# Row fetches of the mixer stage queued behind the vector instruction before them and spaced by 7.5 instead of 11; two kinds of matrix products pinned to their place

## The chip, the cores and the metric

One core of a Trainium2 chip runs the whole program. The metric is the device time of one execution in microseconds (us). The kernel before takes 3400.1 us, the median of 3 runs (3396.47 to 3403.27).

The core has a matrix engine (TensorE, PE in the profile; its weight loads are PEld), a vector engine (VectorE, DVE), an activation engine (ScalarE, ACT), a general engine (GpSimd, POOL) and SyncE (SP), which here issues most DMAs. Each engine works through its own queue in order. What one engine needs of another it waits for by a semaphore. GpSimd issues the indirect DMAs of this kernel, which fetch table rows by an index.

## The reference

One layer on 1024 tokens of width 1024: a mixer (a gated recurrence and a short convolution, merged by gates), and then PEER, a retrieval of single-neuron experts. Cut to what matters here:

```python
x = x + merged @ w_out[l]                       # the mixer's end
h = rmsnorm(x, norm_ffn_g[l])
q = (h @ w_query).reshape(t, 8, 2, 128)
v1, i1 = lax.top_k(q[:, :, 0] . keys1, 16)      # per head, two halves
v2, i2 = lax.top_k(q[:, :, 1] . keys2, 16)
cand_s = v1[..., :, None] + v2[..., None, :]
top_s, top_pos = lax.top_k(cand_s, 16)          # 16 experts a head, 128 a token
idx = take_along_axis(cand_i, top_pos)          # of 16384 experts
gate = softmax(top_s)
act = gelu(einsum('thkd,td->thk', expert_u[idx], h))
out = einsum('thk,thkd->td', gate * act, expert_v[idx])
x = x + out
return rmsnorm(x, norm_final_g)
```

So each token needs 128 rows of `peer_u`, each multiplied with its activation vector and summed, and 128 rows of `peer_v`, each scaled and added up.

## The kernel before

The 1024 tokens are 8 tiles of 128, or 4 groups G0 to G3 of 256. The program has two stages and an end.

The mixer stage. For each group there are generators: `front` (norm, transposes, convolution), `recurrence` (4 head pairs, each with one cumulative scan on VectorE, L574, and the decays on GpSimd, L705 to L709), `gates_a`, `gates_b`, `post` (merge, output projection with its residual add L639, second norm, query projection, the scores and the first top-16) and `picks_of` (the second top-16, the softmax and the expert numbers of a tile). With G2 begins `all_gates`: for the four tiles 2 to 5 it spreads the picked gates over all 16384 experts by one-hot products, eight tokens at a time: four or five wide VectorE instructions (L1000 to L1003) make the operands, and `spread` multiplies them (L976, L977).

The dense stage. Tiles 2 to 5 go through all experts with dense products: `first` (products with the `peer_u` blocks, L296 and L299, gelu, times the gates, L1032), and `second` with the `peer_v` blocks (products L287 to L289 and L1057, sums L1068). The picks of G3 run beside its beginning.

The rows. Tiles 0, 1, 6 and 7 are done by row instead (`gather`): GpSimd issues one indirect DMA (L902) for expert k of 128 tokens at once, 128 rows of 4 KB. For a `u` row block VectorE multiplies it with the activations and sums (L932, with an accumulator read behind it); for a `v` row block it scales and adds (L938). Below, one such fetch with its one VectorE instruction is called a row fetch, and there are 4 x 128 x 2 = 1024 of them. They are put into blocks of 32 experts, the `v` of a block beside the `u` of the next. `gather` yields after every second expert, so a step of it is mostly four row fetches, u, v, u, v. In the mixer stage four buffers (`mem_g`) take the rows, and from the dense stage on there are eight (`mem_e` too). A fetch waits for its buffer, that is for the VectorE instruction that read it four (eight) fetches ago.

What sets the order. `together` runs the generators of the mixer against a clock of its own, which counts the columns of the products traced so far; a generator that yields a number sleeps for so long on that clock. `paced` (L378) steps the rows: one step, then a sleep of `ROW_STEP`, 11.0 of those clock units. `interleave` (L430) deals out the steps that are left over the dense stage, in proportion to the products traced, out of `ROW_STEPS` = 290; it does so within `issue_after(mine[-1])`, which queues the VectorE instructions of the step behind the last VectorE instruction of the dense work. What is still left comes behind the dense stage. A list scheduler then reorders the instructions of each engine by its own idea of when operands are ready; an edge made by `issue_after` or `keep_in_program_order` is an order that it must keep, and no wait on the chip. `issue_after` binds only instructions on the engine of the one that it is given, so the fetches on GpSimd are not bound by it.

Of the kernel before, what the change touches and what calls it, by code (L numbers as in the profile page):

```python
# [22 lines left out]
P = 128  # L23
# [35 lines left out]
W_SHARE = 0.5  # L59
ROWS_AT_ONCE = 4  # L60
T_REC, T_GATES, T_W, T_POST, T_FRONT, T_PICK = 92.0, 6.4, 55.0, 92.0, 170.0, 10.89
T_SOON, T_ROWS, ROW_STEP = 300.0, 1e4, 11.0
FROM = 2
T_GB, T_FIRST = 27, 40.0
ROW_STEPS, T_DENSE = 290, 1330.0
# [60 lines left out]
class Layer:  # L126
# [251 lines left out]
    def paced(self, rows):  # L378

        while 0 not in self.idx:  # L380
            yield 1
        while not self.stop:
            next(rows)
            self.row_steps += 1
            yield ROW_STEP

# [434 lines left out]
    def pick(self, tile_no, top, topi, mem):  # L821

        nc = self.nc
# [55 lines left out]
        yield PICK  # L879
        ps = self.ps()  # L880
        for i, src in enumerate((i12[:, 0], i12[:, 1], gate)):
            nc.tensor.transpose(ps[:, i * P:(i + 1) * P], src, self.ident)

        pt = self.view(self.M.pt_kb + 2 * DENSE.index(tile_no), [4, P, 2], F16)
        pairs = ps[:, :3 * P].unsqueeze(2).broadcast_to([P, 3 * P, 2])
# [71 lines left out]
    def all_gates(self, tiles, last):  # L957

        nc, M = self.nc, self.M
        T = 8  # L960
        while not last.conv:
            yield 1
        ix = self.view(M.ix_kb, [NKEYS], F16)
        nc.vector.tensor_copy(ix, self.iota)
        ix = ix.rearrange("p (k d) -> p k d", d=2).unsqueeze(1).broadcast_to([P, T, NKEYS // 2, 2])
        todo = []

        def spread():

            o2, q0, q1, dst, out = todo.pop(0)  # L970
            for h in range(2):
                ps = self.ps()
                for j in range(4):
                    tk = 4 * h + j
                    o = ps[:, j * P:(j + 1) * P]
                    nc.tensor.matmul(o, o2[:, tk, :], q0[:, tk, :], start=True, stop=False)  # L976
                    nc.tensor.matmul(o, o2[:, tk, :], q1[:, tk, :], start=False, stop=True)  # L977
                nc.scalar.copy(dst[:, :, 4 * h:4 * h + 4].rearrange("p a t -> p t a"),
                               ps.rearrange("p (t a) -> p t a", t=4))
            if out:  # L980
                nc.sync.dma_start(*out)
                yield OUT

        for i_, t in enumerate(tiles):
            while t not in self.pt:
                yield 1
            pt = self.pt[t]
            for tb in range(P // TB):
                stage = M.stage.take([NKEYS, TB])
                for u in range(0, TB, T):  # L990
                    def along(i):
                        t_ = tb * TB + u
                        return pt[:, i, t_:t_ + T, :].unsqueeze(2).broadcast_to([P, T, NKEYS // 2, 2])

                    def twos(x):
                        return x.rearrange("p t (k d) -> p t k d", d=2)

                    o2, o1 = M.o2.take([T, NKEYS], F16), M.o1.take([T, NKEYS], F16)
                    q0, q1 = M.q0.take([T, NKEYS], F16), M.q1.take([T, NKEYS], F16)
                    nc.vector.tensor_tensor(twos(o2), ix, along(1), op=ALU.is_equal)  # L1000
                    nc.vector.tensor_tensor(twos(o1), ix, along(0), op=ALU.is_equal)
                    nc.vector.tensor_tensor(twos(q0), twos(o1), along(2), op=ALU.mult)
                    self.either(Q_SHARE).tensor_tensor(twos(q1), twos(o1), along(3), op=ALU.mult)  # L1003
                    yield SPREAD if todo else 0
                    if todo:
                        yield from spread()
                    todo.append((o2, q0, q1, stage[:, :, u:u + T],
                                 (self.wd[i_ * (P // TB) + tb], stage) if u + T == TB else None))
        yield SPREAD
        yield from spread()  # L1010

    def dense(self, M, n0, n):
# [170 lines left out]
```

## Time and profile before

| | us |
|---|---|
| median of 3 runs | 3400.1 |
| the profiled execution | 3427.02 |
| its span, first to last instruction | 3425.3 |
| PE busy | 2839.6 |
| DVE busy | 2769.9 |
| POOL busy | 1750.8 |
| ACT busy | 999.3 |

The span has three parts, by what the engines do: the mixer stage to about 1686 us, where the first gates of the dense stage are multiplied; the dense stage to 3102 us, where TensorE ends; and the end to 3425 us, in which VectorE still works through row fetches. In a table of stretches the number in brackets behind an engine's busy time is its count of instructions; PEclk is the granted share of TensorE's full clock; then come the mean busy share of the 16 DMA engines and what they moved.

### The profile page before, as it was taken

The page shows a single profiled execution, that of the slowest core. Times are in us where ns is not written, and L with a number is a line of the kernel's source. Part 1 is how long each engine was busy: PE and PEld are TensorE (multiplying, and loading weights), DVE is VectorE, ACT ScalarE, POOL GpSimd, SP SyncE. Part 2 cuts the span into 40 slices and gives each one's busy share as a digit, 9 for nine tenths or more (in the row PEclk, how much of TensorE's full clock was granted, in tenths as well). Part 3 has the DMA queues.
Part 4 walks back from the last instruction along what each step waited for, and adds up shares of the span by engine and source line. Part 5 has one row for each costly group of instructions (what it writes and reads, how often), then busy time and mean ns, then how long its engine had stood idle before and what let it go on. Part 6 is the DMA issues. An engine that isn't in the chain of part 4 may idle for free.

```text
span 3425.3 us, 42902 instructions
## 1 busy us (share of the span) xinstructions
PE 2839.6 (83%) x14956; PEld 2389.3 (70%) x14956; DVE 2769.9 (81%) x5515; ACT 999.3 (29%) x1528; POOL 1750.8 (51%) x1460
## 2 busy tenths in 40 slices
PE   8999998598975799978689999999999999992000
PEld 7887887487864688867578888888888888881000
DVE  2232489868899865789999999999899999989787
ACT  3232232323312354234323333333333333330000
POOL 0001036665546401220467677676677776657875
PEclk9998999798997899988799999999999999996555
DMA  6434558898886754454689999999899999989998
GB/s 199 139 108 122 162 182 294 274 337 310 299 302 211 279 193 145 149 202 157 223 273 354 356 337 344 333 343 336 317 357 337 336 343 341 341 313 335 321 354 297
DMA packets 321721, 938.01 MB, mean 274 GB/s; under 512 B 29280, under 2 KB 103520, under 8 KB 319456
## 3 DMA queue, kind: packets, MB, share of 16 engines
q0 software_dynamic: 147456, 536.94, 43.5%
q1 hardware_dynamic: 174048, 398.32, 34.0%
q8 instruction: 118, 1.93, 0.2%
q14 instruction: 99, 0.81, 0.1%
HBM read 889.01 MB, written 46.14 MB: 273 GB/s over the span
## 4 chain that ended last, share of the span: by engine, by line
PE 61%; DVE 18%; issue 7%; DMA 7%; POOL 5%; ACT 1%; SPq 0%; POOLq 0%; DVEq 0%; ACTq 0%
PE ps L260 16%; PE ps L1057 15%; PE ps L296 13%; PE ps L299 6%; DMA mem_g<-in_peer_v,idx 4%; DVE mem_g L938 3%; DVE mem_g L932 2%; DVE mem_z L864 2%; POOL mem_g L902 2%; DMA mem_g<-in_peer_u,idx 2%; PE ps L740 2%; PE ps L288 2%; PE ps L287 2%; PE ps L289 2%; PE ps L633 1%
## 5 line engine op out<-in xcount | busy, mean ns | idle before, releaser
L260 PE MATMUL ps<-mem_h,mem_w 128*128 128x256 f32 x3584 | 840.7, 392 | 2.1 <-DVE mem_a L516 1.0
L260 PEld LDWEIGHTS ps<-mem_h,mem_w 128*128 128x128 f32 x3584 | 696.4, 197 | 103.9 <-DVE mem_a L516 1.3
L1057 PE MATMUL ps<-mem_v,mem_ph 128*128 128x512 f32 x2304 | 571.8, 398 | 22.4 <-ACT mem_ph L247 13.1
L902 POOL DMA_INDIRECT mem_g<-in_peer_u,idx x324 | 397.0, 1225 | 261.9 <-DVE mem_g L932 120.9
L902 POOL DMA_INDIRECT mem_g<-in_peer_v,idx x308 | 394.1, 1280 | 262.5 <-DVE mem_g L938 163.7
L1057 PEld LDWEIGHTS ps<-mem_v,mem_ph 128*128 128x128 f32 x2304 | 436.3, 190 | 128.2 <-ACT mem_ph L247 14.0
L296 PE MATMUL ps<-mem_ht,mem_s 128*128 128x512 f32 x2048 | 508.1, 390 | 0.2 <-ACT mem_ht L247 0.2
L932 DVE SCALAR_TENSOR_TENSOR mem_g<-mem_g 128x1024 f32<-128x1024 f32 x324 | 429.0, 1327 | 37.0 <-DMA mem_g<-in_peer_u,idx 33.3
L938 DVE SCALAR_TENSOR_TENSOR mem_g<-mem_g 128x1024 f32<-128x1024 f32 x308 | 411.6, 1336 | 51.1 <-DMA mem_g<-in_peer_v,idx 47.5
L296 PEld LDWEIGHTS ps<-mem_ht,mem_s 128*128 128x128 f32 x2048 | 384.2, 188 | 83.6 <-DVE mem_z L1068 0.5
L705 POOL TENSOR_TENSOR mem_y<-mem_y 128x128 f32<-128x128 f32 x96 | 48.3, 504 | 552.7 <-DVE mem_y L574 552.6
L902 POOL DMA_INDIRECT mem_e<-in_peer_v,idx x204 | 267.5, 1311 | 115.8 <-DVE mem_g L938 69.1
L247 ACT ACTIVATE mem_s<-mem_raw 128x512 fp32r<-128x512 f32 x256 | 160.9, 630 | 509.1 <-PE ps L296 489.8
L902 POOL DMA_INDIRECT mem_e<-in_peer_u,idx x188 | 240.1, 1277 | 112.5 <-DVE mem_e L932 61.9
L938 DVE SCALAR_TENSOR_TENSOR mem_g<-mem_e,mem_g 128x1024 f32<-128x1024 f32 x204 | 269.1, 1319 | 17.9 <-DMA mem_e<-in_peer_v,idx 16.1
L299 PE MATMUL ps<-mem_ht,mem_s 128*128 128x512 f32 x1024 | 273.6, 389 | 0.0
L248 POOL TENSOR_TENSOR mem_s<-mem_raw,mem_s 128x512 fp32r<-128x512 f32 x128 | 189.7, 1483 | 140.6 <-ACT mem_s L247 137.2
L932 DVE SCALAR_TENSOR_TENSOR mem_e<-mem_e,mem_g 128x1024 f32<-128x1024 f32 x188 | 242.9, 1297 | 18.0 <-DMA mem_e<-in_peer_u,idx 17.9
L863 POOL TENSOR_TENSOR mem_z<-mem_z 128x800 f32<-128x800 f16 x64 | 124.8, 1950 | 186.9 <-DVE mem_z L861 176.7
L299 PEld LDWEIGHTS ps<-mem_ht,mem_s 128*128 128x128 f32 x1024 | 192.2, 188 | 39.9
L1032 DVE TENSOR_TENSOR mem_z<-mem_z 128x512 f32<-128x512 f32 x128 | 171.7, 1342 | 33.4 <-ACT mem_z L1030 32.8
L247 ACT ACTIVATE mem_ph<-mem_z 128x512 fp32r<-128x512 f32 x128 | 80.9, 632 | 310.6 <-DVE mem_z L1032 303.7
(194 smaller groups left out, 4216.3 us busy)
## 6 DMA issues: line engine op xcount, KB each, us to landing
mem_w<-in_w_in SPq DMA_DIRECT2D x160, 512.0 KB
mem_raw<-in_peer_ut SPq DMA_DIRECT2D x128, 512.0 KB
mem_z<-in_peer_v SPq DMA_DIRECT2D x128, 512.0 KB
mem_w<-in_w_query SPq DMA_DIRECT2D x64, 512.0 KB
wd<-mem_a SPq DMA_DIRECT2D x16, 2048.0 KB
mem_z<-wd SPq DMA_DIRECT2D x32, 1024.0 KB
mem_w<-in_w_out SPq DMA_DIRECT2D x32, 512.0 KB
mem_w<-in_w_conv SPq DMA_DIRECT2D x32, 256.0 KB
```

Source lines behind the costliest of these rows:

```text
L247: self.nc.scalar.activation(hi, src, AF.Copy)
L248: self.either(pool_share).tensor_tensor(lo, src, hi.bitcast(F32), op=ALU.subtract)
L260: self.nc.tensor.matmul(ps, w[:, kk, :], act[:, kk, :], start=kk == 0, stop=kk == k - 1)
L287: mm(ps, lh, rh, start=first, stop=False, **kw)
L296: mm(ps, w[kk][0], act[part][:, kk, :], start=kk == part == 0, stop=False)
L299: mm(ps, w[j][1], act[0][:, j, :], start=False, stop=j == k - 1)
L863: nc.gpsimd.tensor_tensor(pr, eq, ci[:, hd, :].unsqueeze(2).broadcast_to([P, NCAND, TOPK]), op=ALU.mult)
L902: nc.gpsimd.indirect_dma_start(out=r, out_offset=None, in_=a[table], in_offset=bass.IndirectOffsetOnAxis(ap=self.idx[t][:, k:k + 1], axis=0))
L932: nc.vector.scalar_tensor_tensor(u, u, 1.0, h2, op0=ALU.mult, op1=ALU.mult, accum_out=wt[:, k:k + 1])
L938: nc.vector.scalar_tensor_tensor(acc, v, wt[:, k:k + 1], acc, op0=ALU.mult, op1=ALU.add)
L1032: nc.vector.tensor_tensor(gv, gv, w4[c // 4][:, :, c % 4, :], op=ALU.mult)
L1057: nc.tensor.matmul(acc[t][hf], pp[c][i][:, tk], vp[c][:, k, 512 * hf:512 * hf + 512], start=c == 0 and i == 0 and k == 0, stop=c == NKEYS ...
```

## The change

`ROW_STEP` falls from 11.0 to 7.5. Each step of the rows in `paced` now runs within `issue_after(last)`, with `last` the VectorE instruction traced just before. The three transposes of a dense tile's picks (L882 before, L884 after) and the first product of each half of `spread` (L976 before, L978 after) are pinned by `keep_in_program_order` behind the TensorE instruction traced before them.

```diff
-T_SOON, T_ROWS, ROW_STEP = 300.0, 1e4, 11.0
+T_SOON, T_ROWS, ROW_STEP = 300.0, 1e4, 7.5
...
         while not self.stop:
-            next(rows)
+            last = next(i for i in reversed(self.traced()) if i.engine == mybir.EngineType.DVE)
+            with self.tc.issue_after(last):
+                next(rows)
             self.row_steps += 1
             yield ROW_STEP
...
-            nc.tensor.transpose(ps[:, i * P:(i + 1) * P], src, self.ident)
+            self.tc.keep_in_program_order(nc.tensor.transpose(ps[:, i * P:(i + 1) * P], src, self.ident))
...
-                    nc.tensor.matmul(o, o2[:, tk, :], q0[:, tk, :], start=True, stop=False)
+                    mm = nc.tensor.matmul(o, o2[:, tk, :], q0[:, tk, :], start=True, stop=False)
+                    if j == 0:
+                        self.tc.keep_in_program_order(mm)
                     nc.tensor.matmul(o, o2[:, tk, :], q1[:, tk, :], start=False, stop=True)
```

The lines behind L382 move by two, those behind L975 by four (L932 is L934, L938 is L940, L1032 is L1036, L1068 is L1072).

Counted over the whole order of VectorE's queue, row fetches stand as follows (the scans L574 mark the head pairs, four a group):

| row fetches on VectorE | before | after |
|---|---|---|
| ahead of the 7th scan | 7 | 4 |
| 7th to 13th scan | 219 | 148 |
| 13th scan to the first gate product of the dense stage (L1032) | 20 | 200 |
| from there to the last sum of the dense stage (L1068) | 578 | 587 |
| behind it | 200 | 85 |

VectorE's queue behind the 8th scan, in the recurrence of G1. First before, from the end of the decays (L721) on; L750 to L758 are the scores of a head pair, L776 its state:

```order
L721 TENSOR_TENSOR mem_y<-mem_y 128x256
L932 SCALAR_TENSOR_TENSOR mem_g<-mem_g 128x1024
L938 SCALAR_TENSOR_TENSOR mem_g<-mem_g 128x1024
L750 TENSOR_TENSOR mem_y<-ps,c_masks 128x256
L932 SCALAR_TENSOR_TENSOR mem_g<-mem_g 128x1024
L750 TENSOR_TENSOR mem_y<-ps,c_masks 128x256
L938 SCALAR_TENSOR_TENSOR mem_g<-mem_g 128x1024
L776 SCALAR_TENSOR_TENSOR st_126<-st_125,el,ps 64x64 x2
L758 TENSOR_TENSOR mem_y<-mem_y 128x2x32
L932 SCALAR_TENSOR_TENSOR mem_g<-mem_g 128x1024
L758 TENSOR_TENSOR mem_y<-mem_y 128x4x16
L938 SCALAR_TENSOR_TENSOR mem_g<-mem_g 128x1024
```

And the same place now:

```order
L723 TENSOR_TENSOR mem_y<-mem_y 128x256
L752 TENSOR_TENSOR mem_y<-ps,c_masks 128x256 x2
L760 TENSOR_TENSOR mem_y<-mem_y 128x2x32
L760 TENSOR_TENSOR mem_y<-mem_y 128x4x16
L760 TENSOR_TENSOR mem_y<-mem_y 128x8x8
L778 SCALAR_TENSOR_TENSOR st_126<-st_125,el,ps 64x64 x2
L760 TENSOR_TENSOR mem_y<-mem_y 128x16x4
L760 TENSOR_TENSOR mem_y<-mem_y 128x32x2
L760 TENSOR_TENSOR mem_y<-mem_y 128x64
L934 SCALAR_TENSOR_TENSOR mem_g<-mem_g 128x1024 x2
L778 SCALAR_TENSOR_TENSOR st_125<-st_126,el,ps 64x64 x2
```

Six row fetches stood between the pieces of one chain, and now two stand behind them.

VectorE's queue at the first residual adds of G3's `post` (L639, now L641), where the spread of the last dense tiles runs beside it. Before:

```order
L639 TENSOR_TENSOR mem_z<-ps,mem_z 128x512
L864 TENSOR_REDUCE mem_z<-mem_z 128x16
L861 TENSOR_TENSOR mem_z<-iota_x,mem_z 128x800
L1001 TENSOR_TENSOR mem_a<-mem_z 128x1024
L639 TENSOR_TENSOR mem_z<-ps,mem_z 128x512
L1000 TENSOR_TENSOR mem_a<-mem_z 128x1024
L1002 TENSOR_TENSOR mem_o<-mem_a,mem_z 128x1024
L1003 TENSOR_TENSOR mem_o<-mem_a,mem_z 128x1024
```

And now:

```order
L641 TENSOR_TENSOR mem_z<-ps,mem_z 128x512
L1005 TENSOR_TENSOR mem_a<-mem_z 128x1024
L940 SCALAR_TENSOR_TENSOR mem_g<-mem_g 128x1024
L866 TENSOR_REDUCE mem_z<-mem_z 128x16
L863 TENSOR_TENSOR mem_z<-iota_x,mem_z 128x800
L1004 TENSOR_TENSOR mem_a<-mem_z 128x1024
L1006 TENSOR_TENSOR mem_o<-mem_a,mem_z 128x1024
L1007 TENSOR_TENSOR mem_o<-mem_a,mem_z 128x1024
L1004 TENSOR_TENSOR mem_o<-mem_z 128x1024
L934 SCALAR_TENSOR_TENSOR mem_g<-mem_g 128x1024
L641 TENSOR_TENSOR mem_z<-ps,mem_z 128x512
L940 SCALAR_TENSOR_TENSOR mem_g<-mem_g 128x1024
```

Where no row fetch stood, three now stand within these twelve instructions.

TensorE's queue at the transposes of the first dense tile's picks. Before:

```order
L769 MATMUL ps<-mem_y 64x64
L771 MATMUL ps<-mem_y 64x64
L882 MATMUL ps<-c_ident,mem_z 128x128 x3
L260 MATMUL ps<-mem_h_153,mem_w 128x256 x8
L976 LDWEIGHTS mem_a
L976 MATMUL ps<-mem_o,mem_a 128x128
L976 LDWEIGHTS mem_a
L976 MATMUL ps<-mem_o,mem_a 128x128
```

And now:

```order
L771 MATMUL ps<-mem_y 64x64
L773 MATMUL ps<-mem_y 64x64
L884 MATMUL ps<-c_ident,mem_z 128x128 x3
L260 MATMUL ps<-mem_h_153,mem_w 128x256 x8
L978 LDWEIGHTS mem_a
L978 MATMUL ps<-mem_o,mem_a 128x128
L981 LDWEIGHTS mem_a
L981 MATMUL ps<-mem_o,mem_a 128x128
```

The transposes stand at the same place in TensorE's queue (three of the four tiles' have the same number of instructions ahead of them in both kernels, and the second tile's have 28 more). Of the spread's products the two of one token now follow each other, where the first products of several tokens stood together.

## Rows read from the trace of the kernel before

**Rows 1.** The page: busy time of each engine, the span in 40 slices for DVE and the DMA engines, and the chain that ended last by engine.

```profile
PE 2839.6 (83%) x14956; PEld 2389.3 (70%) x14956; DVE 2769.9 (81%) x5515; ACT 999.3 (29%) x1528; POOL 1750.8 (51%) x1460
...
DVE  2232489868899865789999999999899999989787
...
DMA  6434558898886754454689999999899999989998
...
PE 61%; DVE 18%; issue 7%; DMA 7%; POOL 5%; ACT 1%; SPq 0%; POOLq 0%; DVEq 0%; ACTq 0%
```

**Rows 2.** Busy time of the engines by stretch: window, its length, then PE, PEld, DVE, ACT and POOL busy with their counts, PEclk, DMA share, GB/s.

```profile
525.50:1120.00 594.50, 462.96 (x2710) 397.18 (x2709) 520.37 (x1232) 158.92 (x258) 353.27 (x329) 0.87 0.83 291
1120.00:1690.00 570.00, 476.97 (x3236) 415.46 (x3235) 440.65 (x1453) 235.10 (x342) 122.55 (x118) 0.89 0.54 188
1690.00:1800.00 110.00, 99.33 (x414) 79.56 (x412) 109.97 (x124) 33.10 (x48) 75.88 (x52) 0.95 0.80 267
1800.00:3102.00 1302.00, 1302.00 (x5655) 1062.07 (x5654) 1209.37 (x1444) 405.01 (x595) 901.92 (x655) 1.00 0.94 338
3102.00:3425.30 323.30, 0.58 (x3) 0.14 (x1) 264.67 (x351) 6.32 (x13) 233.37 (x196) 0.51 0.90 329
```

**Rows 3.** The same view for single lines on DVE, the mixer's two stretches: first L932 (each instruction counts twice, with its accumulator read), then L938. Columns: window, length, DVE busy (count), PEclk, DMA share, GB/s.

```profile
525.50:1120.00 594.50, 171.70 (x246) 0.87 0.83 291
1120.00:1690.00 570.00, 11.24 (x18) 0.89 0.54 188
...
525.50:1120.00 594.50, 126.67 (x96) 0.87 0.83 291
1120.00:1690.00 570.00, 14.80 (x11) 0.89 0.54 188
```

**Rows 4.** The same view for the end: L932 and L938 from 3104 to 3287.1 us, and then all engines in the two parts of the end.

```profile
3104.00:3287.10 183.10, 73.53 (x120) 0.51 0.92 335
...
3104.00:3287.10 183.10, 70.46 (x55) 0.51 0.92 335
...
3104.00:3287.10 183.10, 0.00 (x0) 0.00 (x0) 151.93 (x231) 4.58 (x10) 144.08 (x114) 0.51 0.92 335
3287.10:3425.30 138.20, 0.00 (x0) 0.00 (x0) 110.74 (x118) 1.38 (x3) 87.90 (x81) 0.50 0.87 323
```

**Rows 5.** The timeline of DVE, single instructions: start, length, engine, line, operation. The 7th and the 13th scan, the first gate product of the dense stage, its last sums, the row fetch behind them, and the row fetch that is the 940th of the 1024.

```profile
525.45 0.73 DVE L574 TENSOR_TENSOR_SCAN mem_y<-keep,mem_y 128x256 f32<-128x256 bf16 x1
...
1119.99 0.68 DVE L574 TENSOR_TENSOR_SCAN mem_y<-keep,mem_y 128x256 f32<-128x256 bf16 x1
...
1686.17 1.27 DVE L1032 TENSOR_TENSOR mem_z<-mem_z 128x512 f32<-128x512 f32 x2
...
3102.33 1.27 DVE L1068 TENSOR_TENSOR mem_z<-mem_z,ps 128x512 f32<-128x512 f32 x2
...
3104.13 1.21 DVE L932 SCALAR_TENSOR_TENSOR mem_e<-mem_e,mem_g 128x1024 f32<-128x1024 f32 x1
...
3287.12 1.22 DVE L932 SCALAR_TENSOR_TENSOR mem_e<-mem_e,mem_g 128x1024 f32<-128x1024 f32 x1
```

**Rows 6.** Busy time by stretch as in rows 2, from scan to scan (the 7th to the 13th), and the last part of the mixer.

```profile
525.50:619.10 93.60, 78.40 (x445) 66.87 (x444) 86.34 (x161) 20.95 (x39) 62.29 (x55) 0.91 0.86 293
619.10:684.10 65.00, 31.69 (x221) 26.79 (x221) 53.48 (x93) 17.56 (x25) 42.99 (x44) 0.63 0.79 267
684.10:771.40 87.30, 82.84 (x474) 70.74 (x473) 60.48 (x114) 21.46 (x33) 54.63 (x54) 0.96 0.91 338
771.40:854.40 83.00, 70.59 (x427) 61.65 (x426) 67.14 (x193) 27.17 (x47) 44.35 (x43) 0.88 0.89 308
854.40:921.40 67.00, 62.20 (x385) 53.74 (x384) 57.67 (x185) 22.97 (x42) 34.37 (x38) 0.92 0.88 311
921.40:1120.00 198.60, 137.24 (x765) 117.39 (x764) 195.25 (x495) 48.82 (x76) 114.64 (x96) 0.86 0.77 264
...
1450.00:1690.00 240.00, 168.41 (x1109) 146.21 (x1109) 213.21 (x718) 97.91 (x136) 51.07 (x31) 0.82 0.54 194
```

**Rows 7.** Waits: who waited, for whom, us in total, times, longest. The first row is PE from 525.5 to 1120 us, the next four PE from 1120 to 1690, then two of DVE and one of POOL from 525.5 to 1120.

```profile
PE ps L882 <- DVE mem_z L878: 35.6, 1, 35.6
...
PE ps L976 <- DVE mem_o L1002: 35.1, 15, 6.4
PE ps L882 <- DVE mem_z L878: 16.7, 2, 13.0
...
PE ps L977 <- DVE mem_z L1003: 4.3, 6, 1.6
PE ps L977 <- DVE mem_o L1003: 2.7, 6, 1.6
...
DVE mem_g L938 <- DMA mem_g<-in_peer_v,idx: 26.0, 26, 2.8
DVE mem_g L932 <- DMA mem_g<-in_peer_u,idx: 18.6, 26, 2.0
...
POOL mem_g L902 <- DVE mem_g L938: 56.4, 37, 6.6
```

**Rows 8.** One line in a stretch: L932 on DVE from 525.5 to 1120 us (ns of one: least, median, longest), and L863 on POOL from 1120 to 1690 us (count, busy us, mean ns, idle before).

```profile
L932 DVE SCALAR_TENSOR_TENSOR mem_g<-mem_g x123: 1193/1218/5777, 526.1 to 1113.9; 128x1024 f32<-128x1024 f32 x123
...
L863 POOL TENSOR_TENSOR mem_z<-mem_z 128x800 f32<-128x800 f16 x25 | 49.2, 1968 | 128.4 <-DVE mem_z L861 124.4 <-DVE sm L854 4.0
```

## Prediction

> **What bounds the kernel now.** I read the page first. VectorE is busy 2770 us of 3425 and TensorE 2840, so neither engine alone explains the span, and the busy shares are means over parts with different limits [rows 1]. The chain that ended last is made of TensorE for 61%, but its end is VectorE, row DMAs and GpSimd. So I cut the span at events of VectorE's timeline [rows 5] and read each piece in the table of stretches [rows 2].
>
> From 1800 to 3102 us, the dense stage, TensorE is busy in every microsecond, 1302 of 1302, at full granted clock, with VectorE at 93% and the DMA engines at 0.94 [rows 2]. TensorE sets its length. From 3102 to 3425 us TensorE does nothing: 323 us in which VectorE, GpSimd and the DMAs work off the 200 row fetches that stand behind the last dense sum. That end is pure row work. In the mixer it is mixed. From the 7th to the 13th scan (525 to 1120 us) VectorE is busy 520 of 594 us, 298 of them with 219 row fetches (L932 123 times, L938 96 times) [rows 2, 3], while TensorE is idle for 132 us. From there to the first dense product (1120 to 1686 us) nearly no row fetches are left, 20 of them [rows 3]: VectorE idles 129 us of 570, TensorE 93, and the DMA share falls from 0.83 to 0.54 [rows 2].
>
> **The end.** 115 fewer row fetches stand behind the dense stage, 85 in place of 200. The fetches come in the same order in both kernels, so the ones that go are the first 115 of the end, and those 85 still to come begin with the 940th. The trace has both moments: the end's first fetch starts at 3104.1 us and the 940th at 3287.1 [rows 5]. Between lie 183.1 us with 60 of L932 and 55 of L938 [rows 4], 1.59 us each, of which VectorE is busy 1.25 (144.0 / 115). TensorE is off in all of it, so nothing hides it: **-183 us**. What follows, 138 us with the last norm, stays. From below, if the remaining fetches ran at 1.25 us each, the end would have held only 144 us for these; as the 183 are measured on the very fetches, I take them.
>
> **The dense stage.** It holds 578 row fetches before and 587 after, nearly the same number within a stage that TensorE fills. Nine more cost VectorE 11 to 12 us, and it has 93 us free there [rows 2]. **0**; if the cover failed, +12.
>
> **The first part of the mixer.** 71 row fetches leave the stretch of 594 us. Their price in it is 298.4 / 219 = 1.36 us of VectorE [rows 3], so up to 97 us go. What is late next is TensorE: a stretch cannot shorten by more than TensorE idles in it. By stretch, with the fetches that go (counted in the two orders, scan to scan): 15, 24, 1, 6, 1, 24, that is 20, 33, 1, 8, 1 and 33 us; TensorE idles 15, 33, 4, 12, 5 and 61 us there [rows 6]. The lesser of the two in each: 15 + 33 + 1 + 8 + 1 + 33 = **-91 us**. In the second of these stretches the granted clock is 0.63, with TensorE busy 49% [rows 6]; if TensorE is kept busier there, that may give a little more. Bounds: -97 (all of it) and -50 (half, if other waits come up). The three fetches that go before the 7th scan stand where TensorE was full, and count nothing.
>
> **The second part of the mixer.** 180 row fetches come in, at 1.36 us 245 us of VectorE. It is busy 441 of 570 us there, which makes 686. From below it grows by 686 - 570 = 116 us (every idle moment filled), from above by the whole 245 (all 129 us of waits for others stay). Where between? In the stretch 921 to 1120 us, where 64 fetches stood beside the spread of the first tiles, VectorE idled only 1.7%; over 525 to 1120 us 12.5%, and in the last 240 us of the mixer 11%, without fetches [rows 6]. With so much more to do its queue is rarely empty; I take the middle of 1.7 and 12.5, 7%: 686 / 0.93 = 738, **+168 us**. The fetches also bring 180 x 0.5 MB = 94 MB to a stretch that moved 107 MB (188 GB/s [rows 2]); over 738 us that is 273 GB/s, below the 291 to 338 that other stretches sustain, so the weight blocks should not come late. On GpSimd a fetch waits for its buffer at most 6.6 us [rows 7], and the decays of a head pair and the sums of `pick` stand behind it in that queue; the recurrence then waits, and with it TensorE. This is the reason why I don't take the lower bound.
>
> **The pinned products.** The transposes keep their place in TensorE's queue in the order, so pinning moves nothing: the 35.6 and 16.7 us that TensorE waited at them [rows 7] were VectorE being late with the picks, and the first goes if 50 fetches less stand ahead, which is in the 91 already. In `spread` the pairs of a token now stand together, so TensorE meets the operand of L1003 one instruction earlier. It waited 7 us for L1003 in the second part, beside 35 for L1002 [rows 7]. In a part that VectorE bounds this is **0**; if it came to count, some 7 us either way, and 35 at most.
>
> **Sum.** -183 + 0 - 91 + 168 + 0 = -106 us. The profiled execution took 3427.0 us (a span of 3425.3) and would take 3321. It is 27 us above the median of the runs; taking the same 106 off the median of 3400.1 gives **3294 us**.
>
> **A rule that speaks against the change.** In rows: L932 takes 1.22 us at the median and 5.78 at the longest between 525 and 1120 us [rows 8], where GpSimd is busy 353 us; with its accumulator read it has a mean of 171.7 / 123 = 1.40 there, and of 73.5 / 60 = 1.23 in the end [rows 3, 4]. A few fetches are thus held up for long, and the price of 1.36 has that in it. In the second part L863 runs 25 times on GpSimd for 1.97 us [rows 8]. The Trainium skill, SBUF — State Buffer, section Who interferes with whom, says that a VectorE instruction with two SBUF inputs contends with a GpSimd instruction that reads SBUF, and that the one behind waits for the whole of the other. By that rule, as far as this trace bears it out, each L863 could hold up a fetch once more; the few long fetches agree with it.
>
> **Rivals.**
>
> 1. *The queue closes up.* All idle time of VectorE in the second part is filled (+116) and the whole 97 us go in the first. For it: 1.7% idle at 921 to 1120 us. Against: VectorE waited 45 us for row landings (26.0 + 18.6) in the first part [rows 7], with four buffers. -183 - 97 + 116 = -164: 3236 us.
> 2. *The waits of the second part stay.* The recurrence and the `post` of G3 are chains through TensorE and ScalarE, and 129 us of waits remain beside the fetches: -183 - 91 + 245 = -29: 3371 us. For it: 11% idle in the last 240 us, with nothing to fill them. Against: the fetches are ready work of another chain.
> 3. *GpSimd holds up the fetches.* The mechanism of the last paragraph: 25 x 1.97 = 49 us on top of the forecast, -57: 3343 us. For it the 5.78 us, against it a median of 1.22.
> 4. *Slower: the chain of G3 takes every fetch in full.* Fetches stand within it (three in twelve instructions at the residual adds); each adds 1.36 and its wait for landing, (26.0 + 18.6) / 219 = 0.20 us, and the GpSimd queue delays the decays. 245 + 200 x 0.2 = +285, while the first part gives back only half (-45), as other waits come up: +240 against -183, **+57: 3457 us**. It decides from the point where the mixer grows by more than 183 us. Against: TensorE and VectorE idle 222 us together in the second part [rows 2], and it needs that none is used.
> 5. *It doesn't do what it says.* For the pinned products that is my forecast already, at no cost. For the fetches the two orders exclude it: the end has 85 in place of 200.
>
> **How the numbers follow.** Forecast 0.58, rival 1 0.17, rival 2 0.13, rival 3 0.05, rival 4 0.07. Likeliest is 3294. The range begins just under rival 1 (3236) and goes to a little above rival 2 (3371), which leaves out rival 4 and the outer halves of 1 and 2: 3230 to 3385. About 0.2%, 7 us, is what a measurement of this kernel can tell from no change. The first four give less than 3393 except for the upper edge of rival 2: faster 0.88, same 0.04, slower 0.08.
>
> **What will show it.** The end, from TensorE's last product to the last instruction, must be near 140 us in place of 323. The dense stage must stay 1410 to 1425 us long, from the first L1036 to the last L1072. The 13th scan must come near 1030 us in place of 1120, and the first L1036 near 1763 in place of 1686. In the second part VectorE must be busy above 90% with a DMA share of about 0.8. I am wrong if the first L1036 comes later than 1870 us (rival 4), if VectorE idles there as long as before (rival 2), or if the dense stage grows because row fetches land late with the DMA engines at 0.94.

## The result, and the profile after

The changed kernel takes 3310.7 us, the median of 4 runs (3307.6 to 3315.1), against 3401.7 us before (3396.5 to 3407.4, the three runs behind the 3400.1 us and one more): a ratio of 0.9733, 95% interval 0.9713 to 0.9753, so 91 us faster. The forecast was 3294, with a range from 3230 to 3385.

The page of the changed kernel, the lines that answer to [rows 1]:

```profile
PE 2836.4 (86%) x14956; PEld 2385.7 (72%) x14956; DVE 2737.9 (83%) x5515; ACT 1004.8 (30%) x1531; POOL 1752.4 (53%) x1460
...
DVE  3233478677899898999999999989999989899998
...
DMA  6443548598874888878758999989999999899998
...
PE 57%; DVE 22%; DMA 8%; issue 6%; POOL 4%; ACT 1%; SPq 0%; DVEq 0%; POOLq 0%; ACTq 0%
```

TensorE, VectorE and GpSimd run as many instructions as before. In the second part of the mixer VectorE's slices 6 5 7 are 9 8 9 now, and the DMA slices 5 4 4 5 4 are 8 8 8 7 8.

The timeline of VectorE at the same events as in [rows 5]: the 13th scan, the first gate product and the last sum of the dense stage.

```profile
1040.52 1.37 DVE L576 TENSOR_TENSOR_SCAN mem_y<-keep,mem_y 128x256 f32<-128x256 bf16 x1
...
1762.40 2.04 DVE L1036 TENSOR_TENSOR mem_z<-mem_z 128x512 f32<-128x512 f32 x1
...
3172.61 1.28 DVE L1072 TENSOR_TENSOR mem_z<-mem_z,ps 128x512 f32<-128x512 f32 x2
```

And the table of stretches between them, as in [rows 2]: the two parts of the mixer, the dense stage, the end.

```profile
525.90:1040.50 514.60, 443.07 (x2678) 381.57 (x2678) 418.28 (x1114) 149.88 (x250) 261.67 (x253) 0.91 0.75 264
1040.50:1762.40 721.90, 489.58 (x3241) 425.35 (x3240) 670.76 (x1753) 250.09 (x357) 361.82 (x306) 0.81 0.79 279
...
1762.40:3173.90 1411.50, 1403.95 (x6088) 1142.55 (x6086) 1305.93 (x1564) 438.05 (x643) 981.87 (x716) 1.00 0.94 337
...
3173.90:3310.60 136.70, 1.79 (x8) 1.13 (x6) 119.91 (x173) 5.98 (x11) 85.40 (x79) 0.52 0.88 332
```

With the kernel before cut at its own events of [rows 5] (the last dense sum ends at 3103.6 us), the end falls from 322 to 137 us, the first part of the mixer from 594 to 515, and the second grows from 566 to 722, with VectorE idle in it 51 us in place of 129. The dense stage is 1411 us long and was 1417.

The row fetches in the two parts, L934 (counted twice, with its accumulator read) and then L940, as in [rows 3]:

```profile
525.90:1040.50 514.60, 111.16 (x176) 0.91 0.75 264
1040.50:1762.40 721.90, 129.66 (x200) 0.81 0.79 279
...
525.90:1040.50 514.60, 82.32 (x60) 0.91 0.75 264
1040.50:1762.40 721.90, 138.14 (x100) 0.81 0.79 279
```

They are 148 and 200, as the order has them. Their price in the second part is (129.66 + 138.14) / 200 = 1.34 us.

The waits of TensorE over both parts of the mixer of the changed kernel, that answer to [rows 7]:

```profile
PE ps L978 <- DVE mem_o L1006: 108.8, 21, 9.3
PE ps L884 <- DVE mem_z L880: 97.7, 3, 44.3
```

TensorE waits more than before at both kinds of pinned products (56 us at L976 and 52 at L882 over both parts before), and it is idle 232 us in the second part, where it was idle 92. VectorE is busy 93% of that part. Its own waits for the landings of row fetches, first over both parts of the mixer and then in the second alone:

```profile
DVE mem_g L934 <- DMA mem_g<-in_peer_u,idx: 25.6, 22, 2.5
DVE mem_g L940 <- DMA mem_g<-in_peer_v,idx: 19.4, 22, 2.5
...
DVE mem_g L934 <- DMA mem_g<-in_peer_u,idx: 6.6, 8, 1.8
DVE mem_g L940 <- DMA mem_g<-in_peer_v,idx: 5.8, 6, 1.9
```

### The profile page after: what moved, and what is told of

Same layout as the page of the kernel before. It is cut to its first block, busy times and chain, and to the rows that moved or that the text cites. A ratio compares the mean times of both kernels' runs of the same rounds, so it can differ in the third digit from the quotient of the medians.

```text
span 3310.6 us, 42876 instructions
## 1 busy us (share of the span) xinstructions
PE 2836.4 (86%) x14956; PEld 2385.7 (72%) x14956; DVE 2737.9 (83%) x5515; ACT 1004.8 (30%) x1531; POOL 1752.4 (53%) x1460
## 4 chain that ended last, share of the span: by engine, by line
PE 57%; DVE 22%; DMA 8%; issue 6%; POOL 4%; ACT 1%; SPq 0%; DVEq 0%; POOLq 0%; ACTq 0%
PE ps L1061 15%; PE ps L296 13%; PE ps L260 11%; PE ps L299 7%; DVE mem_g L940 5%; DVE mem_g L934 3%; DMA mem_g<-in_peer_v,idx 3%; DMA mem_g<-in_peer_u,idx 3%; DVE mem_z L866 2%; PE ps L289 2%; PE ps L288 2%; PE ps L287 2%; PE ps L742 2%; PE ps L635 2%; POOL mem_g L904 2%
## 5 line engine op out<-in xcount | busy, mean ns | idle before, releaser
L904 POOL DMA_INDIRECT mem_g<-in_peer_u,idx x352 | 443.0, 1258 | 395.6 <-DVE mem_g L934 247.0
L904 POOL DMA_INDIRECT mem_g<-in_peer_v,idx x336 | 416.5, 1240 | 327.5 <-DVE mem_g L940 185.4
L940 DVE SCALAR_TENSOR_TENSOR mem_g<-mem_g 128x1024 f32<-128x1024 f32 x336 | 460.4, 1370 | 27.3 <-DMA mem_g<-in_peer_v,idx 23.7
L934 DVE SCALAR_TENSOR_TENSOR mem_g<-mem_g 128x1024 f32<-128x1024 f32 x352 | 453.2, 1293 | 29.7 <-DMA mem_g<-in_peer_u,idx 29.1
L904 POOL DMA_INDIRECT mem_e<-in_peer_v,idx x176 | 233.4, 1326 | 124.6 <-DVE mem_g L940 83.7
L904 POOL DMA_INDIRECT mem_e<-in_peer_u,idx x160 | 209.8, 1312 | 101.1 <-DVE mem_e L934 59.6
L940 DVE SCALAR_TENSOR_TENSOR mem_g<-mem_e,mem_g 128x1024 f32<-128x1024 f32 x176 | 242.9, 1380 | 7.1 <-DMA mem_e<-in_peer_v,idx 5.8
L934 DVE SCALAR_TENSOR_TENSOR mem_e<-mem_e,mem_g 128x1024 f32<-128x1024 f32 x160 | 202.7, 1274 | 0.7 <-DMA mem_e<-in_peer_u,idx 0.6
L248 POOL TENSOR_TENSOR mem_s<-mem_raw,mem_s 128x512 fp32r<-128x512 f32 x128 | 181.8, 1421 | 40.1 <-ACT mem_s L247 37.8
L1036 DVE TENSOR_TENSOR mem_z<-mem_z 128x512 f32<-128x512 f32 x128 | 157.3, 1229 | 44.3 <-ACT mem_z L1034 43.8
L247 ACT ACTIVATE mem_v<-mem_z 128x1024 fp32r<-128x1024 f32 x128 | 128.9, 1053 | 143.9 <-PE ps L289 141.3
```

What stands on the lines that cost most here:

```text
L247: self.nc.scalar.activation(hi, src, AF.Copy)
L248: self.either(pool_share).tensor_tensor(lo, src, hi.bitcast(F32), op=ALU.subtract)
L904: nc.gpsimd.indirect_dma_start(out=r, out_offset=None, in_=a[table], in_offset=bass.IndirectOffsetOnAxis(ap=self.idx[t][:, k:k + 1], axis=0))
L934: nc.vector.scalar_tensor_tensor(u, u, 1.0, h2, op0=ALU.mult, op1=ALU.mult, accum_out=wt[:, k:k + 1])
L940: nc.vector.scalar_tensor_tensor(acc, v, wt[:, k:k + 1], acc, op0=ALU.mult, op1=ALU.add)
L1036: nc.vector.tensor_tensor(gv, gv, w4[c // 4][:, :, c % 4, :], op=ALU.mult)
```

## The experiments

Theory A, behind the forecast: what pays is that row fetches leave the end, where nothing else runs; VectorE's work sets the mixer's length, and where in the mixer the fetches stand matters little. The rivals were that the hold pays (B), that the pins pay or cost (C), that the second part is at its limit (D), that landings, buffers or GpSimd's queue set it (E). All runs below are compared with runs of the kernel before on the same chip.

**The spacing alone, the hold alone, no pins, no hold.** Four kernels on one chip. `e1_step_only` is the kernel before with `ROW_STEP` 7.5:

```diff
-T_SOON, T_ROWS, ROW_STEP = 300.0, 1e4, 11.0
+T_SOON, T_ROWS, ROW_STEP = 300.0, 1e4, 7.5
```

> ROW_STEP 7.5 alone, no hold and no pins. In the order 219 row fetches stay between the 7th and the 13th scan, 126 stand from there to the first dense gate product and 90 behind the dense stage. Theory A (what pays is that fetches leave the end; where in the mixer they stand matters little, since VectorE sets the mixer's length): the first part stays 594 us, the second has 441 + 106 x 1.36 = 585 us of VectorE work, at 94% busy 622 us (+52), the end is 110 x 1.59 = 175 us shorter: about -123 us against before, the same as the changed kernel within 15 us. Theory B (the hold pays, by clearing VectorE for the chains): the first part stays 594 us and the second grows as much as with the hold, +150 us, so about -25 us.

`e2_no_pins` is the changed kernel without `keep_in_program_order`:

```diff
-            self.tc.keep_in_program_order(nc.tensor.transpose(ps[:, i * P:(i + 1) * P], src, self.ident))
+            nc.tensor.transpose(ps[:, i * P:(i + 1) * P], src, self.ident)
...
-                    if j == 0:
-                        self.tc.keep_in_program_order(mm)
```

> The changed kernel without the two pins. Theory A: the same as the changed kernel within 10 us, since TensorE's stalls at the transposes and the spread lie in stretches that VectorE bounds. Theory C (the pins pay): 30 us or more slower than the changed kernel, or, if the pins cost (TensorE waited 98 us at the pinned transposes in the changed kernel against 52 before), 30 us or more faster.

`e3_queue_only` is that with `ROW_STEP` 11.0 again, so the hold alone:

```diff
-T_SOON, T_ROWS, ROW_STEP = 300.0, 1e4, 7.5
+T_SOON, T_ROWS, ROW_STEP = 300.0, 1e4, 11.0
```

> The hold alone, ROW_STEP 11 and no pins. In the order 103 row fetches stand between the 7th and the 13th scan (219 before), 139 from there to the first dense gate product (20 before), 202 behind the dense stage (200 before). Theory A: the first part falls by up to 90 us (limited by TensorE), the second has 441 + 119 x 1.36 = 603 us of VectorE work, at 93% busy 648 us (+78), the end stays: -12 us, within 20. Theory B: the first part falls by 90 us and the second grows by half of that: -40 us or more.

`e4_no_queue` is the changed kernel without the hold:

```diff
-            last = next(i for i in reversed(self.traced()) if i.engine == mybir.EngineType.DVE)
-            with self.tc.issue_after(last):
-                next(rows)
+            next(rows)
```

> ROW_STEP 7.5 and the pins, without the hold. Theory A: as with ROW_STEP alone, within 10 us of it. Theory B: 60 us or more slower than the changed kernel. Theory C: differs from ROW_STEP alone by 30 us or more.

| kernel | us | ratio to before, 95% interval |
|---|---|---|
| spacing alone | 3324.9 | 0.9764 (0.9745 to 0.9783) |
| spacing and hold, no pins | 3318.9 | 0.9747 (0.9728 to 0.9767) |
| hold alone | 3384.2 | 0.9935 (0.9917 to 0.9952) |
| spacing and pins, no hold | 3314.9 | 0.9731 (0.9714 to 0.9748) |
| all three (the change) | 3310.7 | 0.9733 (0.9713 to 0.9753) |

The table of stretches of the spacing alone, first and second part of the mixer and the end:

```profile
526.20:1116.00 589.80, 467.89 (x2729) 401.89 (x2728) 530.03 (x1231) 158.99 (x258) 338.17 (x329) 0.85 0.84 295
1116.00:1756.00 640.00, 488.60 (x3229) 422.42 (x3227) 567.56 (x1625) 240.77 (x348) 250.35 (x225) 0.85 0.72 252
3170.90:3315.40 144.50, 1.74 (x8) 1.08 (x6) 125.58 (x182) 5.96 (x11) 91.23 (x83) 0.52 0.88 332
```

And of the hold alone:

```profile
527.30:1020.70 493.40, 440.98 (x2679) 380.63 (x2678) 359.70 (x1042) 151.44 (x250) 208.97 (x207) 0.92 0.65 224
1020.70:1653.70 633.00, 482.18 (x3251) 418.06 (x3248) 581.89 (x1610) 242.00 (x346) 286.06 (x241) 0.85 0.74 266
3070.40:3377.40 307.00, 1.65 (x8) 0.99 (x6) 264.86 (x351) 6.44 (x13) 215.91 (x196) 0.51 0.93 348
```

And of the spacing with the pins, without the hold:

```profile
525.10:1112.60 587.50, 459.52 (x2707) 394.63 (x2706) 517.36 (x1228) 157.74 (x256) 349.08 (x327) 0.86 0.84 293
1112.60:1751.60 639.00, 488.11 (x3207) 422.34 (x3206) 569.52 (x1634) 237.04 (x344) 249.60 (x229) 0.84 0.73 255
3165.80:3302.00 136.20, 0.71 (x4) 0.23 (x2) 119.75 (x174) 5.98 (x11) 83.73 (x79) 0.51 0.88 331
```

Theory B falls. With 7.5 the spacing alone makes a mixer of 590 + 640 = 1230 us, the whole change one of 515 + 722 = 1237: the hold moves 70 fetches from the first part into the second, and what the first gives the second takes. With 11.0 the hold is worth about 22 us. VectorE's idle time in the second part falls from 127 us (the second trace of before, below) to 51 by it; that this is why it pays there is likely, not shown. The spacing alone is 81 us faster than before, where 123 were expected of theory A: its second part grows by 76 us in place of 52, since VectorE is busy 89% of it and not the 94% that were taken.

The pins are worth nothing that these intervals tell from zero while the hold is there (0.9747 and 0.9733); without it 0.9764 and 0.9731 point to some 11 us, with intervals that just touch. Theory C's 30 us are excluded. Nor do the 11 us, if they are real, come from TensorE's waits in the mixer: of the 13 us between the two traces the mixer has 3 (1229.8 and 1226.5) and the end 8 (144.5 and 136.2), where 90 row fetches stand without the pins and 85 with them.

**The kernel before once more.** `e5_before_again` changes nothing.

> The kernel before, unchanged, for a second trace of it. Its first profiled execution took 3427 us, 20 to 30 us more than its timed runs. If the excess is in the end (200 row fetches in 322 us there, 201 in 307 us in the trace of the hold alone), the end comes to 300 to 310 us here and the other three parts are as in the first trace within 5 us. If it is spread, every part is shorter by about 0.7%.

It gives 3410.3 us, ratio 0.9999 (0.9979 to 1.0019). Its stretches, in the order of [rows 2] (first part, second part, dense stage, end):

```profile
526.80:1124.00 597.20, 468.62 (x2727) 401.86 (x2726) 515.79 (x1231) 159.41 (x258) 353.72 (x329) 0.86 0.83 291
1124.00:1687.60 563.60, 472.82 (x3229) 412.20 (x3227) 436.73 (x1431) 234.00 (x339) 122.90 (x118) 0.89 0.55 189
1687.60:3103.90 1416.30, 1405.24 (x6072) 1144.69 (x6072) 1323.72 (x1593) 440.48 (x645) 980.19 (x709) 0.99 0.93 333
3103.90:3410.50 306.60, 0.00 (x0) 0.00 (x0) 262.46 (x348) 6.32 (x13) 217.20 (x194) 0.50 0.93 345
```

The excess of the first trace sat in the end: 307 us here, 322 there, at the same 262 to 265 us of VectorE work; the DMAs moved 345 GB/s in place of 329. The other parts agree within 3 us. So a fetch in the end costs 1.53 us (306.6 / 200), not 1.59 to 1.61, the last norm counted in; the 115 that went come to (306.6 - 136.7) / 115 = 1.48.

**Closer and wider spacing.** The changed kernel with one number changed, `ROW_STEP` 6.0, 5.0 and 9.0:

```diff
-T_SOON, T_ROWS, ROW_STEP = 300.0, 1e4, 7.5
+T_SOON, T_ROWS, ROW_STEP = 300.0, 1e4, 6.0
```

> The changed kernel with ROW_STEP 6.0. In the order 176 row fetches stand between the 7th and the 13th scan (148 with 7.5), 224 from there to the first dense gate product (200), 37 behind the dense stage (85). Theory A: the first part grows by some 26 us, the second by 24 x 1.36 = 33 us, the end falls by 48 x 1.55 = 74 us: 15 us faster than the changed kernel, ratio to before near 0.969. Theory D (the second part is at its limit, so further fetches cost as much there as in the end or more): the same as the changed kernel or slower.

> The changed kernel with ROW_STEP 5.0. In the order 200 row fetches in the first part of the mixer (148), 235 in the second (200), 7 behind the dense stage (85). Theory A: first part +50, second +48, end -78 x 1.55 = -121 us: 23 us faster than the changed kernel, ratio near 0.966. Theory D: slower than ROW_STEP 6 by 10 us or more.

> The changed kernel with ROW_STEP 9.0. In the order 134 row fetches stand in the first part of the mixer, 163 in the second, 138 behind the dense stage. Measured so far with the hold: both parts of the mixer together 1126 us at 242 fetches, 1236 at 348, 1309 at 400, 1373 at 435, so 1.04, 1.40 and 1.83 us for each further fetch, against about 1.53 in the end. With 297 in the mixer they come to 1126 + 55 x 1.04 = 1183 us (-53 against the changed kernel) and the end to 53 x 1.53 = 81 us more: some 28 us slower than the changed kernel, ratio to before near 0.982. Rival: the price of a fetch in the mixer is flat between the two points no more than up to 300, and 9.0 is as good as 7.5 within 10 us.

The two parts of the mixer and the end, with 6.0, then 5.0, then 9.0:

```profile
525.10:1065.50 540.40, 454.06 (x2690) 390.09 (x2689) 460.72 (x1159) 153.05 (x252) 288.33 (x283) 0.89 0.81 279
1065.50:1833.90 768.40, 484.75 (x3223) 419.94 (x3222) 687.17 (x1782) 240.67 (x347) 388.96 (x327) 0.78 0.79 278
3250.10:3316.10 66.00, 2.13 (x10) 1.38 (x8) 59.96 (x103) 5.74 (x10) 33.95 (x29) 0.56 0.77 292
```

```profile
525.10:1104.60 579.50, 464.50 (x2688) 398.01 (x2688) 484.91 (x1195) 159.32 (x257) 319.81 (x307) 0.86 0.81 282
1104.60:1898.00 793.40, 505.39 (x3234) 434.36 (x3233) 710.76 (x1800) 242.26 (x348) 408.17 (x335) 0.78 0.78 275
3313.90:3344.00 30.10, 1.32 (x6) 0.75 (x4) 24.41 (x74) 5.75 (x10) 0.00 (x0) 0.59 0.37 142
```

```profile
524.80:1041.10 516.30, 451.68 (x2722) 390.17 (x2721) 399.54 (x1094) 147.68 (x248) 252.78 (x238) 0.91 0.73 248
1041.10:1739.10 698.00, 504.05 (x3209) 435.29 (x3209) 623.74 (x1693) 250.31 (x356) 307.92 (x268) 0.81 0.74 261
3158.00:3371.30 213.30, 1.80 (x8) 1.13 (x6) 185.22 (x254) 6.21 (x12) 143.72 (x131) 0.52 0.91 342
```

| ROW_STEP | fetches in the two parts | both parts, us | the end, us | ratio to before, 95% interval |
|---|---|---|---|---|
| 9.0 | 297 | 516.3 + 698.0 = 1214 | 213 | 0.9868 (0.9834 to 0.9901) |
| 7.5 | 348 | 514.6 + 721.9 = 1237 | 137 | 0.9733 (0.9713 to 0.9753) |
| 6.0 | 400 | 540.4 + 768.4 = 1309 | 66 | 0.9744 (0.9709 to 0.9778) |
| 5.0 | 435 | 579.5 + 793.4 = 1373 | 30 | 0.9793 (0.9758 to 0.9827) |

A further fetch in the mixer costs 22 / 51 = 0.4 us between 297 and 348, 72 / 52 = 1.4 between 348 and 400, 64 / 35 = 1.8 beyond, and in the end it saves 1.4 to 1.5 and at last 1.2. Theory D holds from 7.5 on: there the mixer has no cheap place left, and the two prices meet; 7.5 and 6.0 are not told apart by their intervals.

The 0.4 should not be read as the price of all fetches below 348. Each of these points is one trace, and from the hold alone (242 fetches in 1126 us, no pins) to 9.0 a fetch costs 88 / 55 = 1.6 us. Two kernels that differ in the spacing alone give the mean: from the second trace of before (239 fetches, 1161 us) to the spacing alone (345, 1230 us) it is 69 / 106 = 0.65 us, while VectorE's idle time over both parts falls from 208 to 132 us.

Nor do fetches get dear because VectorE is full over the whole mixer. It idles 191 us over both parts with 9.0, 147 with 7.5, 161 with 6.0 and 177 with 5.0: with more fetches than at 7.5 the idle time that is left grows. It is full only in stretches (from 1400 to 1700 us of the changed kernel it is busy 292 of 300), and its waits for landings grow from 45 us with 7.5 to 71 with 6.0 and 100 with 5.0. How much each of the two has in the price was not separated. The waits with 6.0, over both parts:

```profile
DVE mem_g L940 <- DMA mem_g<-in_peer_v,idx: 41.1, 27, 4.3
DVE mem_g L934 <- DMA mem_g<-in_peer_u,idx: 29.9, 29, 3.9
```

I had expected 6.0 and 5.0 to gain 15 and 23 us, since I took VectorE's 1.36 us alone; 9.0 lost more than the 28 us that I reckoned from the hold alone without pins, about 46 (0.0135 of 3415), as the price up to 348 is lower than the 1.04 taken.

**Half the vector work of the mixer's fetches.** `e8_half_mixer`, the changed kernel with

```diff
-                    nc.vector.scalar_tensor_tensor(u, u, 1.0, h2, op0=ALU.mult, op1=ALU.mult,
+                    w_ = D if "e0" in self.regions else D // 2
+                    nc.vector.scalar_tensor_tensor(u[:, :w_], u[:, :w_], 1.0, h2[:, :w_], op0=ALU.mult, op1=ALU.mult,
```

and the same for the `v` rows.

> The changed kernel with the vector instructions of the mixer's row fetches on 512 of the 1024 columns; it leaves out half of those products and sums, while the fetches themselves stay whole. Each such instruction is some 0.55 us shorter. Theory A (VectorE sets the second part of the mixer): that part falls by 80 to 110 us (200 x 0.55), the first by up to 40 us, the rest stays. Theory E (the row fetches' landings, their four buffers or GpSimd's queue set it): the second part falls by less than 30 us.

3247.1 us, ratio 0.9518 (0.9482 to 0.9553). Its first and second part:

```profile
525.30:1018.20 492.90, 448.80 (x2709) 387.46 (x2708) 343.48 (x1112) 146.78 (x246) 229.00 (x255) 0.93 0.78 277
1018.20:1691.00 672.80, 479.45 (x3233) 417.73 (x3232) 555.71 (x1743) 245.56 (x352) 310.07 (x301) 0.82 0.83 298
```

The second part falls by 49 us, between the two theories, while VectorE loses 115 us of work there. Its waits in that part, for landings:

```profile
DVE mem_g L942 <- DMA mem_g<-in_peer_v,idx: 29.6, 22, 4.3
DVE mem_g L935 <- DMA mem_g<-in_peer_u,idx: 25.5, 17, 4.5
```

55 us, where the changed kernel waits 12 us for them in that part. So VectorE's work is not all that sets the second part: 115 us less of it make the part 49 us shorter, and 43 us more go into waits for landings, which stand close behind.

**Three row buffers.** `e10_three_buffers`:

```diff
-        self.rows = self.ring(300, 4, 4)
+        self.rows = self.ring(300, 4, 3)
```

> The changed kernel with three row buffers in the mixer in place of four (seven in place of eight from the dense stage on). Theory A (VectorE's own work sets the second part, landings matter only beside it): the second part grows by less than 30 us. Theory E (with half of the vector work VectorE waited 55 us for landings in that part, with all of it 12, so landings are close behind): it grows by 60 us or more, and the first part by 20 or more.

3392.8 us, ratio 0.9940 (0.9918 to 0.9962). First and second part:

```profile
527.50:1073.80 546.30, 452.46 (x2679) 388.66 (x2678) 423.67 (x1115) 150.93 (x249) 252.16 (x256) 0.88 0.74 249
1073.80:1834.20 760.40, 488.09 (x3224) 421.94 (x3223) 673.22 (x1748) 241.70 (x349) 340.06 (x303) 0.79 0.76 264
```

VectorE's waits for landings over both parts:

```profile
DVE mem_g L940 <- DMA mem_g<-in_peer_v,idx: 65.7, 43, 6.2
DVE mem_g L934 <- DMA mem_g<-in_peer_u,idx: 53.0, 40, 2.7
```

32 us more in the first part and 38 in the second, at nearly the same VectorE work: one buffer less takes most of the gain back. The 70 us agree with the growth of the waits for landings, from 45 us in the changed kernel to 119. Theory E is right for the first part; the 38 us of the second lie between the two theories. More than four buffers were not tried, so what a fifth would give is open.

**A share of the gate products on GpSimd.** `e11_gpsimd_share`:

```diff
-Q_SHARE = 0
+Q_SHARE = 0.25
```

> The changed kernel with every fourth of the q1 products of the gates' spread (L1007, 64 of them at 0.8 us) on GpSimd in place of VectorE, 16 in all. Theory A: VectorE has 13 us less in the mixer, 10 us faster. Theory F (GpSimd's queue, in which the fetches stand, and its contention with VectorE cost more than that): 5 us or more slower.

3338.7 us, ratio 0.9783 (0.9751 to 0.9815): about 17 us slower than the changed kernel. The second part of the mixer and the moved products:

```profile
1040.30:1789.90 749.60, 497.08 (x3240) 430.98 (x3239) 684.44 (x1739) 242.20 (x351) 389.49 (x322) 0.79 0.77 268
```

```profile
L1007 POOL TENSOR_TENSOR mem_z<-mem_a,mem_z 128x1024 f16<-128x1024 f16 x15 | 30.0, 1998 | 10.2 <-DVE mem_y L760 4.2 <-PE ps L981 4.0 <-DVE mem_a L1005 1.7
```

VectorE is busy 684 us there in place of 671 although it has 15 products less, and waits 31 us for landings in place of 12. The intervals just touch, and the second part alone is 28 us longer: Theory F rather than A. The trace shows both contention and later landings. The 200 fetches' own instructions take 12 us more (21 of them last over 1.5 us, where 15 did) and L1004 takes 9 us more, against 11 us that L1007 has less; and the landings cost 19 us more. Why they come later was not separated.

No version tried that does the whole work beats the changed kernel beyond the intervals.

## Why the prediction was right, point by point

Both the direction and the size came out, 91 us measured and 106 forecast, and the mechanism is the one forecast: the end and the first part of the mixer give more than the second part takes back. By terms, against the second trace of before (and the first in brackets):

| term | forecast | measured |
|---|---|---|
| the end | -183 | -170 (-185) |
| the dense stage | 0 | -5 (-6) |
| first part of the mixer | -91 | -83 (-80) |
| second part | +168 | +158 (+156) |
| up to the 7th scan | 0 | -1 (0) |
| sum | -106 | -100 (-115) |

The two traces differ by 100 us, the medians of the runs by 91; single executions of the kernel before range from 3396 to 3427 us, so 9 us between a pair of traces and a pair of medians is not explained further.

*The end* agrees with the trace it was read from (183 and 185), and is 13 us too large against the second one: it was read from one execution in which the end was 15 us longer than in the other trace. That the fetches that go were measured themselves didn't help, as they were measured once. The reading of what goes there was right: 85 fetches remain, in 137 us (140 forecast).

The two terms of the mixer are each off by 8 to 12 us, the first part too favourable and the second too dear. They cancel: +77 forecast for both, +75 and +76 measured. That their sum is so close, and with it the moment of the first gate product, is luck.

*The first part*: the lesser of VectorE's gain and TensorE's idle time gave 91 and it was 80 against the trace it was read from. One step in it was wrong: the wait at the first tile's transposes, of which I said that it goes with 50 fetches less ahead of it, is still 28 us (it was 36); TensorE waits there for VectorE's picks as before:

```profile
PE ps L884 <- DVE mem_z L880: 27.9, 1, 27.9
```

The 13th scan came at 1040.5 us (1030 forecast).

*The second part*: 7% idle was taken, the middle between 1.7 and 12.5, and it is 51 of 722, 7.1%. The middle had no reason of its own, and other orders idle more there (8% with the hold alone, 11% with the spacing alone or with 6.0), so this hit is in part luck. 686 us of VectorE work were reckoned, and 671 are there, 2% less: 738 us forecast for the part, 722 measured. The first gate product stands at 1762.4 us, 1763 forecast. The half-work run shows that VectorE's work counts there, but at 49 us for 115, and that the landings, which I had only against rival 1, are the next.

*The pinned products* at 0: no effect that the runs tell from zero beside the hold. TensorE's waits at the transposes grew from 52 us to 98 and cost nothing visible: without the pins the two parts are 1237 us long, as with them. Nor did the hold pay with 7.5, which the forecast had not valued apart.

Rival 1 (the queue closes up) and rival 2 (the waits stay) bracket it as meant. None of the signs of being wrong showed: the first L1036 came before 1870 us, VectorE idles 51 us in place of 129, and the dense stage did not grow. Rival 3, GpSimd holding up fetches, happened at a smaller size: the price of 1.34 in the second part against 1.25 in the end [rows 4] is 0.09 x 200 = 18 us, in the forecast's price already. In the trace 15 of the 200 instructions last over 1.5 us, each of them beside a GpSimd product; the 161 with none beside them take 1.24 us in the mean. The line of the changed kernel's second part, and one case in its timeline:

```profile
L934 DVE SCALAR_TENSOR_TENSOR mem_g<-mem_g x100: 1194/1214/2934, 1066.5 to 1710.2; 128x1024 f32<-128x1024 f32 x100
```

```profile
1471.34 1.80 POOL L865 TENSOR_TENSOR mem_z<-mem_z 128x800 f32<-128x800 f16 x1
1471.65 2.57 DVE L934 SCALAR_TENSOR_TENSOR mem_g<-mem_g 128x1024 f32<-128x1024 f32 x1
```

The fetch's instruction begins 0.3 us after GpSimd's, and takes 2.57 us in place of 1.21. By the Trainium skill, SBUF — State Buffer, section Who interferes with whom, a VectorE instruction with two SBUF inputs contends with a GpSimd instruction that reads SBUF. These two rows agree.

## What to carry to other kernels

Work that stands alone behind the last busy stage costs its full price there (1.48 us a fetch); moved beside a stage with idle time of the engine that it needs, it costs less, here 0.65 us a fetch in the mean from 239 to 345 of them. It stops paying before that engine's idle time is used up: beyond 348 fetches each costs about as much as in the end or more, with 147 us of VectorE's time in the mixer still idle. So read the idle time of the needed engine in the stage that is to take the work, don't count on filling all of it, and stop where the two prices meet. Where the engine that bounds a stage works in order, shifting its work about within the stage may only move the time about with it, as the hold did with 7.5; with 11.0 the hold gained 22 us.

## What had not been expected

The end of one and the same program took 322 us in one execution and 307 in another, with equal VectorE work and 329 against 345 GB/s: this stretch, which row DMAs feed, differed by 5%, where the program's executions lie within 1%. And one buffer of 512 KB less cost 70 us over the two parts of the mixer, although VectorE had waited only 45 us in all for landings with four: it waits 119 us with three.
